# One 512-column matmul for a weight's high part: FFN-in, q/k and gate products with two sums a bank, joined afterwards

## The chip, the core and the metric

The kernel runs on one core of a Trainium2 chip. A core has a matrix engine (PE, with its weight loads shown as PEld), a vector engine (DVE), an activation engine (ACT), GpSimd (POOL), a sync engine that issues the DMAs (SP) and 16 DMA engines. PE writes its sums to eight banks (PSUM), from where ACT and DVE read them. Each engine works its own instructions off in the order in which they stand and waits for the others by semaphores. The metric is the device time of one execution in microseconds, the median of three runs.

## The reference

A trunk of two layers over 256 tokens with 1024 features. Each layer has three sub-layers: a SwiGLU feed-forward (FFN) of width 2816, a mixer of three kinds of attention with gates, and a second FFN. All inputs are float32, and each sub-layer's input is normed, scaled and shifted by vectors that a product of the conditioning vector with `w_ada` gives (adaLN).

```python
h = pre(x, 0)                                   # norm, scale, shift
x = x + 0.5*mod[:,0,2] * swiglu(h, wg, wu, wd)  # (silu(h@wg) * (h@wu)) @ wd
h = pre(x, 1)
(q.., k.., v.., g_sb, g_dil, g_swa) = split(h @ w_in)
merged = sigmoid(g_sb)*(o_sb@w_br_sb) + sigmoid(g_dil)*(o_dil@w_br_dil) + sigmoid(g_swa)*(o_swa@w_br_swa)
x = x + mod[:,1,2] * (merged @ w_out)
h = pre(x, 2)
x = x + 0.5*mod[:,2,2] * swiglu(h, wg2, wu2, wd2)
```

## The kernel before, in words

Every product of float32 operands is made of three: a number is split in a high part of type float32r and a low part, the rest. A product is weight-high by row-high, weight-low by row-high, and weight-high by row-low. The rows' parts are `hH` and `hL`, the weights' are `wH` and `wL`.

The weights stream in as loads of 1 MB, three buffers of them (`RAWS`). A load is cut in units; a unit is a [1024, 128] block of weight columns for FFN-in, q/k and gates. For each unit ACT casts the high part (L149) and DVE subtracts to get the low part (L157). `feed` splits units up to `AHEAD` = 5 in front of the products, and there are `NB` = 6 slots, so a cast also waits until PE is done with the unit six before it.

`step` (L564) writes the program for one unit: first `feed` (the split of the unit five ahead), then adaLN's steps if some are due (L282 on DVE, L280 on ACT, from two load buffers), then the unit's matmuls, then what the unit before left (`pending`), then the unit's own `post`. ACT and DVE get their instructions in this order.

`aform` (L580) makes the matmuls of a unit: eight blocks of 128 features, for each a 256-column matmul with the high and one with the low weight part, then eight more with the rows' low part: 24 of 256 columns. In an FFN, gate and up products of one block of 128 columns share a bank, half each; after the up unit ACT takes the silu of the gate half (L647), DVE multiplies it with the other half (L648), and a step later ACT casts and DVE subtracts the result's parts for the down product (L651, L652). Units go gate, gate, up, up. The first two units of an FFN (other than the first FFN, which has a start of its own, L608) put their products with the rows' low part last.

In the mixer two q/k units share a bank and ACT copies it (L838). Two gate units share a bank and ACT takes the tanh of it (L866). Between the gate units stand the pieces of the attention heads, by a list in `run_mixer`: scores on PE (`pa`, `pb`, `pc`), bias and maxima on DVE (L1046, L1051, L1056), exponentials on ACT (L1066, L1072), division on DVE (L1081, L1088), transposes on PE (`pt`, L1100). After two or four gate units a branch's output product follows (`pb`), and DVE multiplies it with the tanh (L887 to L891).

The down and output products (L701, `pd`) take the tokens as the stationary operand and move 512 or 256 columns of a weight. The six sub-layers are numbered 0 to 5; 1 and 4 are mixers.

Of the kernel before, what the change touches and what calls it, by code (L numbers as in the profile page):

```python
# [16 lines left out]
P = 128  # L17
# [12 lines left out]
# slots of split units, how many of them are split ahead, and slots of loads  # L30
# [3 lines left out]
# units at the end of a sub-layer whose products go piece by piece, and those that the first norm's transposes follow  # L34
# [16 lines left out]
# the last rows' columns on the vector engine; the activation engine takes the others  # L51
# [11 lines left out]
def shape_constants():  # L63
    """One-hot of the bucket of each distance, and the mask of each head by distance (distance 255 - index)."""
# [16 lines left out]
class Unit:  # L81
    """A piece of a weight: `view` picks it from the raw tile of load `raw`; `pe` runs its products."""
# [6 lines left out]
class Trunk:  # L89
# [23 lines left out]
    # ---------------------------------------------------------------- weight stream  # L113
# [23 lines left out]
    def feed(self, ahead=AHEAD, high=0):  # L137
        """Split the units that lie up to `ahead` in front of the products, H one step before L."""
# [26 lines left out]
    # ---------------------------------------------------------------- adaLN  # L165
    def ada_setup(self):
# [11 lines left out]
        # after which sub-layer a sum is reduced, while the next norm runs; the others as they are complete  # L178
# [6 lines left out]
    def first_load(self, q):  # L185
        """Two blocks of columns of the first shift and scale, into what the feed-forward takes later."""
        t = self.sp.tile([P, KB, 2, 256], F32, tag=("bigA", "bigB")[q % 2], name=f"first{q}", bufs=1)
        for kb in range(KB):
            src = self.a["w_ada"][0, kb * P:(kb + 1) * P, 0:2 * D].rearrange("p (c n) -> p c n", c=2)
            self.nc.sync.dma_start(t[:, kb], src[:, :, 256 * q:256 * q + 256])  # L190
        self.first_src[q] = t

    def first_mac(self, q, kbs):
        """Products of some blocks of rows with the vector, on the vector engine."""
# [9 lines left out]
    def first_sum(self, q, kbs, acc=False):  # L204
        """Sums over the rows, of products made here or before: a column tile each for the two blocks of the shift
        and of the scale."""
# [22 lines left out]
    def first_h(self, q, xt, out):  # L229
        """The first norm's output, two blocks of features."""  # L230
# [95 lines left out]
    def ada_reduce(self, ch):  # L326
        """Sums over the partitions on the tensor engine; returns what is left to do.

        A gate is wanted along the free dimension: ones times the products. Shift and scale are wanted along the
        partitions: four column tiles sum a quarter of the columns each, and transposes turn the rows."""  # L330
# [39 lines left out]
    # ---------------------------------------------------------------- constants  # L370
# [69 lines left out]
    # ---------------------------------------------------------------- norm  # L440
    def square(self, t, cols, tag):
        """Mean square over some of the columns."""
# [37 lines left out]
    def norm_pe(self, t, s, xn):  # L480
        """Features to the partitions, one half of them a bank."""
# [9 lines left out]
    def norm_evac(self, t, s, ps, between=()):  # L491
        """Scale and shift by feature, one engine a bank; the high parts too."""
# [33 lines left out]
    def alloc_h(self, s):  # L526
        self.hH = self.sp.tile([P, KB, S], F32R, tag="hH", name=f"hH{s}", bufs=1)
        self.hL = self.sp.tile([P, KB, S], F32R, tag="hL", name=f"hL{s}", bufs=1)
# [11 lines left out]
    def final_gain(self, t, sl):  # L540
        """x times the gain, while the mean square is summed."""
# [21 lines left out]
    # ---------------------------------------------------------------- unit lists  # L563
# [16 lines left out]
    def aform(self, u, out, xh, xl, off=0, part="all"):  # L580
        """out += W^T x for one block of 128 columns of the unit; the products with the low part of x come last."""
# [8 lines left out]

    def col_raw(self, src, widths=((0, 256),)):
        """Load of columns of a [1024, n] weight as [128, 8, 256]."""
# [8 lines left out]
    def plan_ffn(self, l, i, s):  # L601
# [5 lines left out]
        def start_pe(b0, q):  # L607
            """Two blocks of columns over two of rows; both sums of a block share a bank."""  # L608
# [22 lines left out]
        def gate_pe(fb):  # L631
            def pe(u, part="all"):
                if part != "low":
                    ps[fb] = self.ps(f"pf{s}_{fb}")
                self.aform(u, ps[fb][:, :S], self.hH, self.hL, part=part)
            return pe

        def up_pe(fb):
            return lambda u: self.aform(u, ps[fb][:, S:], self.hH, self.hL)

        def up_post(fb):
            def post():
# [6 lines left out]

                def later():  # L650
                    nc.scalar.copy(self.ffH[:, fb, :], f32)  # L651
                    nc.vector.tensor_tensor(self.ffL[:, fb, :], f32, self.ffH[:, fb, :], op=ALU.subtract)  # L652
                return later
# [18 lines left out]
        for q in range(3 if s == 0 else 0, NF // 2):  # L672
            rg, ru = self.col_raw(wg, ((q * 256, 256),)), self.col_raw(wu, ((q * 256, 256),))
            for r, mk in ((rg, gate_pe), (ru, up_pe)):
                for b in range(2):
                    fb = 2 * q + b
                    view = lambda t, b=b: t.rearrange("p (k n) -> p k n", k=KB)[:, :, b * P:(b + 1) * P]
                    u = Unit(r, view, (KB, P), mk(fb), up_post(fb) if r == ru else None)
# [5 lines left out]
    def plan_rows(self, w, nk):  # L684
        """Units of one block of 128 rows of a [n, 1024] weight, two a load."""
# [657 lines left out]
```

## Time and profile before

| what | value |
|---|---|
| median of 3 runs | 1215.85 us (1215.71 to 1215.98) |
| span of the profiled execution | 1213.2 us |
| PE busy | 1184.2 us, 98%, 9005 matmuls |
| DVE busy | 830.4 us, 68% |
| ACT busy | 615.6 us, 51% |
| HBM traffic | 238 GB/s over the span |

The span runs from the first to the last instruction; the rest of a run's time lies around it. The profile's busy time of a matmul contains its way through the array, so that matmuls overlap: how fast they follow one another is read from their starts.

### The profile page before, as it was taken

How to read it: one execution, taken by the hardware profiler on the slowest of the kernel's cores; microseconds unless marked ns; L12 is line 12 of the kernel's file. 1: busy time of each engine (PE TensorE's matmuls, PEld its weight loads, DVE VectorE, ACT ScalarE, POOL GpSimd, SP SyncE). 2: the span in 40 equal slices, each digit the busy share in tenths (PEclk: the TensorE clock that was granted, in tenths of full speed). 3: DMA queues.
4: the chain of work that ended last, by engine and by line, in shares of the span. 5: the costliest groups of instructions: out<-in, count | busy, mean ns of one | idle time of the engine just before them, and what ended most of it. 6: DMA issues, size and time to landing. Idle time of an engine off the chain costs nothing.

```text
span 1213.2 us, 21570 instructions
## 1 busy us (share of the span) xinstructions
PE 1184.2 (98%) x9005; PEld 1115.3 (92%) x9005; DVE 830.4 (68%) x1075; ACT 615.6 (51%) x953; POOL 17.5 (1%) x38
## 2 busy tenths in 40 slices
PE   6999999899999999999999999999999999999997
PEld 5999987799999999999889999889999998999986
DVE  3677576777889897766577667557766788555544
ACT  5555343546564475444365444346655446444432
POOL 1000000000000000000000000000000000000000
PEclk9999999899999999999999999999999999999999
DMA  9999999698779859877739776758843584656550
GB/s 318 308 307 328 266 328 321 205 299 286 249 241 312 310 186 330 253 243 249 251 112 300 217 243 226 257 157 282 269 153 114 180 273 149 199 184 198 174 173 35
DMA packets 189673, 287.58 MB, mean 237 GB/s; under 512 B 6806, under 2 KB 155496, under 8 KB 189576
## 3 DMA queue, kind: packets, MB, share of 16 engines
q1 hardware_dynamic: 187656, 279.88, 69.7%
q0 software_dynamic: 1776, 6.14, 1.8%
q8 instruction: 70, 1.15, 0.4%
q14 instruction: 27, 0.22, 0.1%
q10 hardware_dynamic: 144, 0.20, 0.0%
HBM read 285.12 MB, written 3.42 MB: 238 GB/s over the span
## 4 chain that ended last, share of the span: by engine, by line
PE 85%; DMA 6%; DVE 4%; issue 2%; ACT 2%; POOL 0%; SPq 0%; POOLq 0%; ACTq 0%; DVEq 0%
PE pf L589 36%; PE pd L701 18%; PE pg L589 11%; PE pq L589 7%; DMA ada<-in_w_ada 5%; PE pf L619 3%; PE pb L589 3%; PE pv L934 2%; DVE acc L282 1%; DVE wL L157 1%; PE psn L487 1%; PE adag L343 1%; DMA first<-in_w_ada 1%; DMA raw<-in_w_ffn_gate 0%; ACT wH L149 0%
## 5 line engine op out<-in xcount | busy, mean ns | idle before, releaser
L157 DVE TENSOR_TENSOR wL<-raw,wH 128x1024 fp32r<-128x1024 f32 (+1 forms) x384 | 461.9, 1211 | 223.2 <-ACT wH L149 222.8
L149 ACT CAST wH<-raw 128x1024 fp32r<-128x1024 f32 (+1 forms) x384 | 393.1, 1041 | 243.9 <-PE pd L701 94.7
L589 PE MATMUL pf<-hH,wH 128*128 128x256 f32 x1312 | 323.0, 284 | 0.4 <-DVE hH L504 0.4
L589 PE MATMUL pf<-hH,wL 128*128 128x256 f32 x1312 | 322.0, 283 | 0.0
L589 PEld LDWEIGHTS pf<-hH,wH 128*128 128x128 f32 x1312 | 251.8, 192 | 1.7 <-issue 0.9
L589 PEld LDWEIGHTS pf<-hH,wL 128*128 128x128 f32 x1312 | 251.8, 192 | 0.2 <-issue 0.2
L589 PE MATMUL pf<-hL,wH 128*128 128x256 f32 x1312 | 183.7, 283 | 0.0
L282 DVE SCALAR_TENSOR_TENSOR acc<-ada,sc,acc 128x1024 f32<-128x1024 f32 x112 | 143.4, 1280 | 43.6 <-DMA ada<-in_w_ada 43.5
L589 PEld LDWEIGHTS pf<-hL,wH 128*128 128x128 f32 x1312 | 169.0, 192 | 0.0
L701 PE MATMUL pd<-wL,ffH 128*128 128x512 f32 (+1 forms) x440 | 154.6, 351 | 3.5 <-DVE wL L157 3.5
L701 PE MATMUL pd<-wH,ffH 128*128 128x512 f32 (+1 forms) x440 | 154.6, 351 | 0.0
L701 PE MATMUL pd<-wH,ffL 128*128 128x512 f32 (+1 forms) x440 | 153.6, 349 | 0.0
L701 PEld LDWEIGHTS pd<-wL,ffH 128*128 128x128 f32 x440 | 83.8, 191 | 15.3 <-DVE wL L157 4.7
L589 PE MATMUL pg<-hH,wH 128*128 128x256 f32 x384 | 96.0, 288 | 0.0
L701 PEld LDWEIGHTS pd<-wH,ffH 128*128 128x128 f32 x440 | 84.0, 191 | 12.2 <-issue 0.8
L589 PE MATMUL pg<-hH,wL 128*128 128x256 f32 x384 | 94.0, 283 | 0.0
L701 PEld LDWEIGHTS pd<-wH,ffL 128*128 128x128 f32 x440 | 83.6, 190 | 11.0
L647 ACT ACTIVATE sil<-pf 128x256 f32<-128x256 f32 x88 | 33.4, 383 | 96.6 <-PE pf L589 96.6
L589 PEld LDWEIGHTS pg<-hH,wH 128*128 128x128 f32 x384 | 73.4, 191 | 2.3 <-issue 1.3
L589 PEld LDWEIGHTS pg<-hH,wL 128*128 128x128 f32 x384 | 73.4, 191 | 0.0
L648 DVE TENSOR_TENSOR f<-pf,sil 128x256 f32<-128x256 f32 x88 | 36.9, 422 | 32.9 <-ACT sil L647 32.9
L589 PE MATMUL pq<-hH,wH 128*128 128x256 f32 x224 | 55.8, 287 | 0.0
(204 smaller groups left out, 1390.5 us busy)
## 6 DMA issues: line engine op xcount, KB each, us to landing
ada<-in_w_ada SPq DMA_DIRECT2D x128, 512.0 KB, 5.6
raw<-in_w_ffn_down SPq DMA_DIRECT2D x44, 1024.0 KB, 5.0
raw<-in_w_in SPq DMA_DIRECT2D x42, 1024.0 KB, 6.6
raw<-in_w_ffn_gate SPq DMA_DIRECT2D x41, 1024.0 KB, 6.7
raw<-in_w_ffn_up SPq DMA_DIRECT2D x41, 1024.0 KB, 6.0
first<-in_w_ada SPq DMA_DIRECT2D x32, 256.0 KB, 6.0
raw<-in_w_out SPq DMA_DIRECT2D x8, 1024.0 KB, 6.9
raw<-in_w_ffn_gate SPq DMA_DIRECT2D x12, 256.0 KB, 6.0
```

Source lines behind the costliest of these rows:

```text
L149: nc.scalar.copy(u.H, u.view(self.raw_tiles[u.raw]))
L157: nc.vector.tensor_tensor(u.L, u.view(self.raw_tiles[u.raw]), u.H, op=ALU.subtract)
L282: self.nc.vector.scalar_tensor_tensor(acc, src, sc, acc, ALU.mult, ALU.add)
L343: nc.tensor.matmul(ps[h], self.ones, acc[:, h * 512:(h + 1) * 512], start=True, stop=True)
L487: self.nc.tensor.transpose(p[:, i * P:(i + 1) * P], xn[:, fb * P:(fb + 1) * P], self.ident)
L589: nc.tensor.matmul(out, w[:, kb, cs], x[:, kb, :], start=i == 0, stop=i == n - 1)
L619: self.nc.tensor.matmul(ps[fb][:, S * up:S * up + S], w[:, 2 * k + up, b * P:(b + 1) * P], x[:, 2 * q + k, :], start=q == 0 and not up and ...
L647: nc.scalar.activation(sil, p[:, :S], AF.Silu)
L648: nc.vector.tensor_tensor(f32, p[:, S:], sil, op=ALU.mult)
L701: self.nc.tensor.matmul(out, x[:, kb, sl], w[:, 0, hs], start=first and i == 0, stop=last and i == 2)
L934: self.nc.tensor.matmul(out, x[:, 4 * (i % 2) + k, sl], w[:, k, :], start=i % 2 == 0 and j == 0, stop=i % 2 == 1 and j == n - 1)
```

## The change

The rows' high and low parts now stand side by side in one tile, `hHL`, so that a weight's high part meets [high | low] as one 512-column matmul into a whole bank. The weight's low part times the rows' high part goes on as a 256-column matmul into the bank's first half. A unit then has 8 matmuls of 512 columns and 8 of 256, and two sums in its bank, which `join` adds: ACT copies the second half out, DVE adds the first half. Each unit has a bank of its own and a `post` of its own. This is done for FFN-in (except the first FFN's start), q/k and gates; values, branch outputs, down and output products stay. The first two units of the later FFNs keep 24 matmuls of 256 columns, into two sums. In a gate's post the silu and in the mixer the tanh of two gate units follow the join. (Comments are dropped as well; those lines are left out here.)

```diff
     def alloc_h(self, s):
-        self.hH = self.sp.tile([P, KB, S], F32R, tag="hH", name=f"hH{s}", bufs=1)
-        self.hL = self.sp.tile([P, KB, S], F32R, tag="hL", name=f"hL{s}", bufs=1)
+        self.hHL = self.sp.tile([P, KB, 2, S], F32R, tag="hHL", name=f"hHL{s}", bufs=1)
+        self.hH, self.hL = self.hHL[:, :, 0, :], self.hHL[:, :, 1, :]
...
+    def wide(self, u, bank, part="all"):
+        nc = self.nc
+        one, both = bank[:, :S], bank[:, :]
+        k = u.shape[0]
+        seq = []
+        for kb in range(k):
+            if part == "all":
+                seq += [(both, u.H, self.hHL[:, kb]), (one, u.L, self.hH[:, kb, :])]
+            elif part == "high":
+                seq += [(one, u.H, self.hH[:, kb, :]), (one, u.L, self.hH[:, kb, :])]
+            else:
+                seq += [(bank[:, S:], u.H, self.hL[:, kb, :])]
+        n = len(seq)
+        for i, (out, w, x) in enumerate(seq):
+            kb = i if part == "low" else i // 2
+            rhs = x.rearrange("p c n -> p (c n)") if part == "all" and i % 2 == 0 else x
+            nc.tensor.matmul(out, w[:, kb, :], rhs, start=part != "low" and i == 0, stop=part != "high" and i == n - 1,
+                             skip_group_check=True)
+
+    def join(self, out, bank):
+        self.nc.scalar.copy(out, bank[:, S:])
+        self.nc.vector.tensor_tensor(out, bank[:, :S], out, op=ALU.add)
...
-                self.aform(u, ps[fb][:, :S], self.hH, self.hL, part=part)
+                self.wide(u, ps[fb], part)
             return pe
 
+        def gate_post(fb):
+            def post():
+                sil = self.sil[:, fb % 3, :]
+                self.join(sil, ps[fb])
+                self.nc.scalar.activation(sil, sil, AF.Silu)
+            return post
+
         def up_pe(fb):
-            return lambda u: self.aform(u, ps[fb][:, S:], self.hH, self.hL)
+            def pe(u):
+                ps[fb] = self.ps(f"pu{s}_{fb}")
+                self.wide(u, ps[fb])
+            return pe
+
+        def up_wide_post(fb):
+            def post():
+                f32 = self.f32[:, fb % 3, :]
+                self.join(f32, ps[fb])
+                self.nc.vector.tensor_tensor(f32, f32, self.sil[:, fb % 3, :], op=ALU.mult)
+                return split(fb, f32)
+            return post
...
-                    u = Unit(r, view, (KB, P), mk(fb), up_post(fb) if r == ru else None)
+                    u = Unit(r, view, (KB, P), mk(fb), post(fb))
...
             for u in us:
                 u.pe(u, "low")
+                u.post()
...
         def qk_pe(i):
             def pe(u):
-                if i % 2 == 0:
-                    ps[i // 2] = self.ps(f"pq{s}_{i}")
-                self.aform(u, ps[i // 2][:, (i % 2) * S:(i % 2 + 1) * S], self.hH, self.hL)
+                ps[i] = self.ps(f"pq{s}_{i}")
+                self.wide(u, ps[i])
...
+                self.join(self.qk[:, i, :], ps[i])
...
         def g_post(b, f):
             def post():
-                if f % 4 == 1:
+                if f % 4 == 0:
                     th[b, f // 4] = self.work([P, 4, S], f"th{s}_{b}_{f}")
-                i = f // 2
-                self.nc.scalar.activation(th[b, f // 4][:, 2 * (i % 2):2 * (i % 2) + 2, :],
-                                          gps[b, i].rearrange("p (b n) -> p b n", b=2), AF.Tanh, scale=0.5)
+                t = th[b, f // 4]
+                self.join(t[:, f % 4, :], gps[b, f])
+                if f % 2:
+                    two = t[:, f % 4 - 1:f % 4 + 1, :]
+                    self.nc.scalar.activation(two, two, AF.Tanh, scale=0.5)
             return post
```

The first place is ACT in the FFN-in part of sub-layer 2, column blocks 12 and 13 (`pf` gate, `pu` up). Before, one silu stands for each pair of a gate and an up unit:

```order
L647 ACTIVATE sil2_4787<-pf2_12_5586 128x256
L149 CAST wH158_5674<-raw85_5517 128x1024
L651 CAST ffH2_4785<-f322_4788 128x256
L647 ACTIVATE sil2_4787<-pf2_13_5617 128x256
L149 CAST wH159_5709<-raw85_5517 128x1024
```

Now the same engine at the same blocks reads:

```order
L615 COPY sil2_4392<-pf2_12_5075 128x256
L669 ACTIVATE sil2_4392<-sil2_4392 128x256
L149 CAST wH156_5097<-raw84_4963 128x1024
L615 COPY sil2_4392<-pf2_13_5101 128x256
L669 ACTIVATE sil2_4392<-sil2_4392 128x256
L149 CAST wH157_5121<-raw84_4963 128x1024
L615 COPY f322_4393<-pu2_12_5127 128x256
L149 CAST wH158_5147<-raw85_5018 128x1024
L688 CAST ffH2_4390<-f322_4393 128x256
L615 COPY f322_4393<-pu2_13_5154 128x256
```

The silu has moved from the up unit to the gate unit, behind a copy; it reads the tile that DVE's add writes, and the cast of the next unit's high part stands behind it.

The second place is DVE at the same blocks, now (an add L616 for each unit, a product L682 for each up unit):

```order
L616 TENSOR_TENSOR sil2_4392<-pf2_12_5075,sil2_4392 128x256
L157 TENSOR_TENSOR wL156_5099<-raw84_4963,wH156_5097 128x1024
L616 TENSOR_TENSOR sil2_4392<-pf2_13_5101,sil2_4392 128x256
L157 TENSOR_TENSOR wL157_5123<-raw84_4963,wH157_5121 128x1024
L616 TENSOR_TENSOR f322_4393<-pu2_12_5127,f322_4393 128x256
L682 TENSOR_TENSOR f322_4393<-f322_4393,sil2_4392 128x256
L157 TENSOR_TENSOR wL158_5149<-raw85_5018,wH158_5147 128x1024
```

Before, these blocks had four splits L157 and two products L648 here, and no add. Now a split stands right behind each add, and its `wH` comes from a cast that stands behind the silu of that add.

The third place is ACT in the gate part of the first mixer, at the second branch's first two gate units (`swa1` is the last group of heads). Before:

```order
L149 CAST wH102_3761<-raw54_3508 128x1024
L866 ACTIVATE th1_1_1_3794<-pg1_1_0_3716 128x512
L1101 COPY pT1_swa0_3796<-pt1_swa0_0_3797 128x384
L1072 ACTIVATE p1_swa1_3750,sm1_swa1_3755<-p1_swa1_3750,sm1_swa1_3755 128x256 x3
L1074 ACTIVATE sm1_swa1_3755<-sm1_swa1_3755 128x6
L149 CAST wH103_3819<-raw55_3615 128x1024
```

Now, on DVE, at the same units:

```order
L1104 TENSOR_SCALAR sm1_swa1_3444<-sm1_swa1_3444 128x6
L157 TENSOR_TENSOR wL102_3452<-raw54_3219,wH102_3450 128x1024
L282 SCALAR_TENSOR_TENSOR acc3_0_3367<-ada74_3369,sc_97,acc3_0_3367 128x1024
L616 TENSOR_TENSOR th1_1_0_3427<-pg1_1_1_3459,th1_1_0_3427 128x256
L157 TENSOR_TENSOR wL103_3504<-raw55_3314,wH103_3502 128x1024
L616 TENSOR_TENSOR th1_1_0_3427<-pg1_1_2_3506,th1_1_0_3427 128x256
```

ACT's row of tanh, transposed copies, exponentials and cast is as before, but for two copies more; the tanh now reads what the add L616 writes, which stands behind a split and an adaLN step on DVE. Before, it read the bank that PE wrote.

## Rows read from the trace of the kernel before

**Rows 1.** The page's first part: busy time of the engines.
```profile
PE 1184.2 (98%) x9005; PEld 1115.3 (92%) x9005; DVE 830.4 (68%) x1075; ACT 615.6 (51%) x953; POOL 17.5 (1%) x38
```

**Rows 2.** Busy time by stage: stretch, length, engines, PE clock, DMA share, GB/s.
```profile
145.00:220.00 75.00, 71.46 (x405) 61.04 (x405) 53.76 (x56) 29.91 (x36) 0.00 (x0) 0.95 0.92 325
300.00:405.00 105.00, 104.75 (x867) 100.78 (x866) 94.65 (x128) 58.32 (x104) 0.00 (x0) 1.00 0.81 275
432.00:559.00 127.00, 127.00 (x1059) 126.98 (x1058) 94.25 (x118) 68.19 (x101) 0.00 (x0) 1.00 0.80 267
626.00:753.00 127.00, 127.00 (x1058) 126.91 (x1057) 88.48 (x112) 65.66 (x99) 0.00 (x0) 1.00 0.74 239
886.00:989.00 103.00, 103.00 (x854) 99.96 (x855) 73.23 (x108) 55.64 (x100) 0.00 (x0) 1.00 0.52 168
1017.00:1144.00 127.00, 127.00 (x1057) 126.94 (x1058) 77.20 (x100) 64.49 (x97) 0.00 (x0) 1.00 0.60 191
```

**Rows 3.** The chain that ended last, in order of time: start, us, what.
```profile
124.56 19.34 DMA ada<-in_w_ada
...
325.44 0.04 DVE p_dil L1081
...
326.73 1.18 PE pt_dil L1100 x9
...
432.18 126.82 PE pf L589 x1056
```

**Rows 4.** Timeline of PE in sub-layer 2's down product: start, us, instruction.
```profile
591.26 0.39 PE L701 MATMUL pd<-wH,ffL 128*128 128x512 f32 x1
591.49 0.28 PE L701 MATMUL pd<-wH,ffH 128*128 128x256 f32 x1
591.60 0.28 PE L701 MATMUL pd<-wL,ffH 128*128 128x256 f32 x1
...
592.08 0.28 PE L701 MATMUL pd<-wH,ffL 128*128 128x256 f32 x1
592.20 0.40 PE L701 MATMUL pd<-wH,ffH 128*128 128x512 f32 x1
```

**Rows 5.** Groups by line and shape: busy us, mean ns, idle before.
```profile
L157 DVE TENSOR_TENSOR wL<-raw,wH 128x1024 fp32r<-128x1024 f32 x372 | 451.6, 1223 | 218.3 <-ACT wH L149 217.9
L149 ACT CAST wH<-raw 128x1024 fp32r<-128x1024 f32 x372 | 384.3, 1050 | 242.5 <-PE pd L701 94.7 <-PE pf L589 62.8 <-issue 23.6
...
L648 DVE TENSOR_TENSOR f<-pf,sil 128x256 f32<-128x256 f32 x88 | 36.9, 422 | 32.9 <-ACT sil L647 32.9
...
L866 ACT ACTIVATE th<-pg 128x512 f32<-128x512 f32 x24 | 14.3, 596 | 41.3 <-PE pg L589 40.1 <-issue 1.2
```

**Rows 6.** Timeline of DVE in sub-layer 2's FFN-in.
```profile
489.53 1.28 DVE L282 SCALAR_TENSOR_TENSOR acc<-ada,sc,acc 128x1024 f32<-128x1024 f32 x1
490.73 0.42 DVE L652 TENSOR_TENSOR ffL<-f,ffH 128x256 fp32r<-128x256 f32 x1
491.06 0.42 DVE L648 TENSOR_TENSOR f<-pf,sil 128x256 f32<-128x256 f32 x1
491.40 1.21 DVE L157 TENSOR_TENSOR wL<-raw,wH 128x1024 fp32r<-128x1024 f32 x1
492.53 0.42 DVE L652 TENSOR_TENSOR ffL<-f,ffH 128x256 fp32r<-128x256 f32 x1
```

**Rows 7.** Timeline of ACT, sub-layer 2's FFN-in.
```profile
487.04 0.38 ACT L647 ACTIVATE sil<-pf 128x256 f32<-128x256 f32 x1 [1.78 <-PE pf L589]
487.32 1.04 ACT L149 CAST wH<-raw 128x1024 fp32r<-128x1024 f32 x1
```

**Rows 8.** Timeline of ACT in the first mixer's gate part, two places.
```profile
319.05 0.94 ACT L1066 ACTIVATE p_dil<-p_dil,sm_dil 128x768 f32<-128x768 f32 x1 [2.31 <-DVE sm_dil L1051]
...
320.58 1.03 ACT L149 CAST wH<-raw 128x1024 fp32r<-128x1024 f32 x1
...
350.74 0.51 ACT L1072 ACTIVATE p_swa<-p_swa,sm_swa 128x256 f32<-128x256 f32 x1 [0.83 <-DVE sm_swa L1059]
...
353.49 1.98 ACT L149 CAST wH<-raw 128x1024 fp32r<-128x1024 f32 x2
```

More of the change, by code (lines that the diff above doesn't have):

```diff
@@ L634, in pe, with split, later @@
                     ps[fb] = self.ps(f"pf{s}_{fb}")
-                self.aform(u, ps[fb][:, :S], self.hH, self.hL, part=part)
+                self.wide(u, ps[fb], part)
             return pe
-        def up_pe(fb):
-            return lambda u: self.aform(u, ps[fb][:, S:], self.hH, self.hL)
+        def gate_post(fb):
[4 more added lines that the diff above has]
+            return post
+        def up_pe(fb):
+            def pe(u):
[9 more added lines that the diff above has]
+            return post
+        def split(fb, f32):
+            def later():
+                self.nc.scalar.copy(self.ffH[:, fb, :], f32)
+                self.nc.vector.tensor_tensor(self.ffL[:, fb, :], f32, self.ffH[:, fb, :], op=ALU.subtract)
+            return later
         def up_post(fb):
@@ L648, in post @@
                 nc.vector.tensor_tensor(f32, p[:, S:], sil, op=ALU.mult)
[L650 to L653, printed above, removed]
+                return split(fb, f32)
             return post
@@ L673, in plan_ffn @@
             rg, ru = self.col_raw(wg, ((q * 256, 256),)), self.col_raw(wu, ((q * 256, 256),))
-            for r, mk in ((rg, gate_pe), (ru, up_pe)):
+            for r, mk, post in ((rg, gate_pe, gate_post), (ru, up_pe, up_wide_post)):
                 for b in range(2):
@@ L826, in pe, with qk_post @@
             def pe(u):
-                if i % 2 == 0:
-                    ps[i // 2] = self.ps(f"pq{s}_{i}")
-                self.aform(u, ps[i // 2][:, (i % 2) * S:(i % 2 + 1) * S], self.hH, self.hL)
+                ps[i] = self.ps(f"pq{s}_{i}")
+                self.wide(u, ps[i])
             return pe
-        def qk_post(q):
+        def qk_post(i):
             def post():
                 nc = self.nc
-                p = ps[q]
-                dst = self.qk[:, 2 * q:2 * q + 2, :]
-                src = p.rearrange("p (b n) -> p b n", b=2)
-                nc.scalar.copy(dst, src)
-                if q == 6:
-                    nc.scalar.copy(self.qk[0:64, 14, :], p[64:128, S:])
-                    nc.scalar.copy(self.qk[64:128, 14, :], p[0:64, S:])
+                self.join(self.qk[:, i, :], ps[i])
+                if i == 13:
+                    nc.scalar.copy(self.qk[0:64, 14, :], self.qk[64:128, 13, :])
+                    nc.scalar.copy(self.qk[64:128, 14, :], self.qk[0:64, 13, :])
             return post
@@ L846, in plan_mixer @@
             for b in range(2):
-                u = Unit(r, half(b), (KB, P), qk_pe(2 * q + b), qk_post(q) if b else None)
+                u = Unit(r, half(b), (KB, P), qk_pe(2 * q + b), qk_post(2 * q + b))
                 self.units.append(u)
@@ L855, in pe @@
             def pe(u):
[L856 to L858 removed]
+                gps[b, f] = self.ps(f"pg{s}_{b}_{f}")
+                self.wide(u, gps[b, f])
             return pe
@@ L909, in plan_mixer @@
                     f = f0 + i
-                    u = Unit(r, half(i), (KB, P), g_pe(b, f), g_post(b, f) if i else None)
+                    u = Unit(r, half(i), (KB, P), g_pe(b, f), g_post(b, f))
                     self.units.append(u)
```

3 lines of the change are left out of this document (removed).

## The prediction, made blind

> **What bounds the kernel now.** I read the page's busy times first: PE is busy 98% of the span, DVE 68%, ACT 51% [rows 1]. Then the stages, because DVE's share is an average: in FFN-in parts PE is busy all the time and DVE 77 to 94 of 127 us, but in the first mixer's gate part DVE is busy 94.65 of 105 us, in the second's only 73.23 of 103 [rows 2]. Then the chain of waits. In an FFN-in part it is one piece of PE, 1056 matmuls in 126.82 us, so 120.1 ns from start to start [rows 3]. In the first sub-layer it goes through adaLN's loads (19.34 us in one piece), with the DMA engines at 0.92 [rows 2, 3]. In the first mixer's gate part it passes through DVE's division L1081 at 325.44 and from there to PE's transposes at 326.73 [rows 3]: there DVE already hands over just in time. So the kernel is bound by PE, except in the first sub-layer (DMA) and at the start of the first mixer's gates (DVE).
>
> **What the change removes on PE.** Converted are 158 FFN-in units (32 in sub-layer 0, 42 in each of 2, 3 and 5), 28 of q/k and 48 of gates, 234 in all, each of eight feature blocks. A block had three 256-column matmuls, 3 x 120.1 = 360.3 ns [rows 3]; now it has one of 512 and one of 256, in turn. The down product shows each handover: a 512 followed by a 256 takes 0.23 us, a 256 that comes behind a 512 takes 0.11, and a 256 before a 512 takes 0.12 [rows 4]. The pair is 0.34 to 0.35 us; I take 0.345, a saving of 15 ns a block, 0.12 us a unit, 5.1 us for 42 units, 28 us for all 234. The ends: the times are read to 10 ns, so 0.35 + 0.01 (nothing saved) to 0.34 (20 ns, 37 us for all).
>
> The Trainium skill weighs less: "TensorE: Matmul & The Clock Gate", section Back-to-back issue gap, gives a warm gap of N/2.4 + 2.5 ns for an isolated matmul, an estimate from it being 109.2 ns for 256 columns and 215.8 for 512, so 2.6 ns saved a block and under 5 us in all. The trace disagrees with its level (120.1 and 230 ns), so the sum goes by the rows.
>
> **What it adds.** One ACT copy and one DVE add of 128x256 a converted unit (240 with the two unconverted units of sub-layers 2, 3, 5). No such copy or add from a bank is in the FFN-in of before; the nearest are the silu from a bank, 0.38 us [rows 7], and the product with a bank half, 0.42 us [rows 5]. I take these. Back to back, DVE's instructions follow one another faster than they last: the adaLN step 1.20 us, the split 1.13, a 128x256 one 0.33 to 0.34 [rows 6]; ACT's silu gives way after 0.28 [rows 7].
>
> ACT's copies are cheap: ACT is half idle. What counts is the new wait. Before, the silu and the tanh waited for PE alone. Now each waits for DVE's add, and behind it in ACT's queue stands the cast `wH` of the unit five ahead, for which DVE's very next instruction, the split, waits. So after the add of a gate unit DVE stands idle: silu 0.28, cast 1.05 [rows 5, 7], with two handovers of about 0.03. One round of four units (gate, gate, up, up), when DVE and ACT set the pace: from first to second gate's add 0.31 + 1.08 + split 1.13 + add 0.42, about 2.95 us; from there to the first up's add the same; product 0.37; then split, `ffL`, add and product, 1.13 + 0.33 + 0.45 + 0.34; split, `ffL` and add of the next round, 1.13 + 0.33 + 0.42. Sum 10.4 us, against PE's 4 x 8 x 0.345 = 11.04 (11.53 before). AdaLN's steps come on top.
>
> The splits run five units ahead. In step, `wL` of the unit five ahead is ready about 3.5 us after the unit before ended (copy 0.38, add 0.42, silu 0.28, cast 1.05, split 1.22, handovers), and is needed 5 x 2.76 = 13.8 us after it. So DVE may fall 10.3 us behind before PE waits.
>
> **By stage.**
> - FFN-in of sub-layer 5: no adaLN step. 10.5 rounds x 10.4 = 109.2 on DVE, 115.9 on PE. PE sets the pace: -5.
> - Sub-layer 3: DVE was 88.48 - 77.20 = 11.3 us busier than in sub-layer 5 [rows 2], adaLN's steps. 120.5 against 115.9: 4.6 behind, inside the lead: -5.
> - Sub-layer 2: 94.25 - 77.20 = 17.1 [rows 2]. 126.3 against 115.9: 10.4 behind, the whole lead. I take 2 us of waits: -3. If the round lasts 0.8 us longer than I have it, this becomes +5 and sub-layer 3 about -3.
> - First mixer, gates, 24 units: DVE's 94.65 us [rows 2] plus 24 adds x 0.34 = 8.1; plus 12 tanhs, each with DVE idle for tanh 0.50 to 0.60, cast 1.05 and handovers, 1.65 [rows 5]: 19.8. At four of them the exponentials of a head group stand between tanh and cast, 1.53 us twice and 2.75 twice [rows 8]: 8.6. Before, ACT did these while DVE split. Sum 131 us against 105. The lead doesn't swallow it: PE's transposes come two units behind DVE's division and already met it with nothing to spare [rows 3], and at the end the output product waits for the last splits and the residual behind them. Less 1 us for the branch units' shorter casts: +25, q/k part included, where DVE has room. Ends: +12 if half the idle stretches are filled by what DVE still has to do, +33 if the stalls bring PE below its clock and the w_out rows wait too.
> - Second mixer: few adaLN steps, 73.23 + 8.1 + 28.4 = 109.7 us [rows 2] against PE's 103 - 2.9 = 100.1: 9.6 behind, within the lead but for the transposes. Gates 0, q/k -1.7, the output rows +2.7: +1 (-4 to +8).
> - Sub-layer 0: bound by DMA [rows 2, 3], so PE's 3.9 us are not seen, and late splits free the load buffers later: +2 (-2 to +8).
> - Norms, values and sub-layer ends: same instructions in the same order, 0.
>
> Sum +25 + 1 + 2 - 3 - 5 - 5 = +15 us on a span of 1213.2, so 1228.2; the runs shown lie 2.65 us over the span (1215.85), which gives 1231.
>
> **Rivals.**
> - *The lead swallows it.* The place is the first mixer's gate part. If DVE's idle stretch after a tanh were under about 0.8 us, its sum there, (94.65 + 8.1 + 12 x 0.8), would lie within 10.3 us of PE's 102; then PE's saving would show everywhere but in sub-layer 0: 202 units x 0.12 = 24 us, 1192. For it: PE is busy 104.75 of 105 us there with DVE 90% busy [rows 2]. Against: the order puts a cast of 1.05 us behind every tanh.
> - *Half of it.* Idle stretches lie partly on existing waits; the mixer costs 12: 1218.
> - *No saving on PE.* If a 512-column matmul with its load costs what two of 256 do, sub-layers 3 and 5 give 0, 2 gives +2, the second mixer +4, the first mixer +25, sub-layer 0 +2: +33, 1249. Against it: 0.23 + 0.11 [rows 4]. The Trainium skill's rule above would come near this: about 1246.
> - *Nothing to see.* Saving and stalls cancel, 1216: the stalls would have to be 10 us in the first mixer.
>
> **How the numbers follow.** Chances: the forecast (1222 to 1240) 0.52; half of it 0.14; no saving or longer rounds (1240 to 1255) 0.17; swallowed (1190 to 1210) 0.11; cancelled 0.06. What a measurement can tell from no change is about 0.2%, 2.4 us. Faster: 0.11 and some of the two middle cases, 0.15; same 0.08; slower 0.77. The range 1212 to 1249 leaves out the swallowed case and the upper end of the no-saving case, together about 0.2.
>
> **What would show it.** Right: in FFN-in, pairs of matmuls start 0.34 to 0.35 us apart; DVE's idle before L157 is still put down to ACT's `wH`, with 1.4 us or more after each add of a gate; PE stalls of several us before the transposes in the first mixer, which ends some 25 us later, while FFN-in of sub-layers 3 and 5 shrinks by 5. Wrong: PE without gaps in the first mixer's gates (then the first rival), or FFN-in parts of sub-layer 5 as long as before (then no saving).

## The result, and the profile after

The changed kernel takes 1269.05 us (median of 4 runs, 1267.91 to 1269.21) against 1215.78 us for the kernel before in the same rounds (1215.18 to 1215.98): 1.0437 times as long, 95% interval 1.0423 to 1.0452. The forecast was 1231 us, with a range up to 1249. The sign was right and the size was not: +53 us, where +15 was forecast.

The page's first part, beside [rows 1]:

```profile
PE 1192.6 (94%) x7133; PEld 1022.8 (81%) x7133; DVE 909.1 (72%) x1315; ACT 675.9 (53%) x1179; POOL 18.1 (1%) x38
```

PE's share falls from 98% to 94%: it waits. DVE's busy time grows by 79 us. Where the time went is read from marks, the first start of the matmul `adag` (L343 in both kernels) at the end of sub-layers 0 to 4 (four more `adag` at 119 us, inside sub-layer 0, are left out); the stages s0 to s5 lie between the marks, and the last one ends with the span. This table of stage lengths is worked out from those starts, for the kernel before in us and for every other kernel as the difference to it, each from its profiled execution:

```
                   s0     s1     s2     s3     s4     s5    span
before           228.6  198.5  193.7  193.7  197.7  201.0  1213.2
forecast            +2    +25     -3     -5     +1     -5     +15
after            +17.7  +28.8   +3.8   -2.3   +7.0   -2.0   +53.0
e1_late           +3.5   +1.8   -2.1   -2.2   -2.5   -2.1    -3.6
e2_join_only     +18.6  +26.5   +3.7    0.0   +8.0   +0.2   +57.0
e3_wide_only      -2.0   -2.7   -2.2   -2.2   -2.5   -2.2   -13.8
e4_s0_before      +0.3  +28.4   +3.8   -2.2   +6.9   -2.1   +35.1
e5_one_op        +25.1  +35.6  +14.6   +7.6  +11.8   -2.0   +92.7
e6_late_group     +7.6   +2.2   -3.5   -3.6   -3.2   -3.5    -4.0
e7_late_s0_g      -1.4   +2.0   -2.2   -2.2   -2.5   -2.2    -8.5
e8_late_group_s0  -2.4   -0.2   -3.5   -3.6   -3.2   -3.5   -16.4
e9_no_ada         +3.4   +2.7   -2.2   -2.3   +3.7   -2.6    +2.7
```

From s2 on, stages that should be alike agree within about 0.1 us between kernels (s5 of e9_no_ada is 0.5 off). s0 and s1 move by up to 3 us: e4, e7 and e8 have the same FFN-in of sub-layer 0 and show +0.3, -1.4 and -2.4. Why is not traced, so a difference of that size in s0 or s1 shows nothing. Each row is one execution: those of e6_late_group and e9_no_ada lie at the upper end of their runs (1210.92 of 1206.45 to 1210.92 us; 1217.58 of 1210.15 to 1218.93), those of e7_late_s0_g and e8_late_group_s0 at the lower end. Of the 38 us by which the forecast fell short, s0 has 15.7.

The windows of the changed kernel: FFN-in of sub-layer 0, the first mixer's gates, its output rows, then FFN-in of sub-layers 2, 3 and 5 (columns as in [rows 2]):

```profile
60.00:155.00 95.00, 89.59 (x492) 74.72 (x490) 65.97 (x98) 46.63 (x87) 1.68 (x2) 1.00 0.84 266
317.00:440.00 123.00, 108.79 (x675) 93.89 (x672) 93.17 (x141) 58.56 (x120) 0.00 (x0) 0.94 0.64 215
440.00:474.00 34.00, 29.36 (x133) 23.56 (x132) 27.06 (x38) 16.49 (x29) 0.74 (x2) 0.85 0.76 259
478.00:608.00 130.00, 127.39 (x727) 109.32 (x726) 101.46 (x152) 75.98 (x137) 0.00 (x0) 1.00 0.73 240
676.00:801.00 125.00, 125.00 (x724) 109.21 (x723) 96.39 (x148) 73.84 (x135) 0.00 (x0) 1.00 0.68 227
1072.00:1197.00 125.00, 124.95 (x721) 109.28 (x722) 91.39 (x143) 79.70 (x142) 0.00 (x0) 1.00 0.58 189
```

The first and third of these stretches in the kernel before:

```profile
60.00:155.00 95.00, 95.00 (x778) 93.27 (x777) 65.95 (x86) 44.85 (x71) 1.68 (x2) 1.00 0.95 301
404.00:427.00 23.00, 23.00 (x130) 20.08 (x129) 17.39 (x24) 10.10 (x18) 0.74 (x2) 1.00 0.75 259
```

In sub-layers 3 and 5 PE is busy without a gap, as it was [rows 2], and the stages are 2.0 to 2.3 us shorter. In the gates PE is idle for 14 of 123 us, at a mean granted clock of 0.94. In the output rows about the same matmuls (133 against 130) take 34 us instead of 23, at a mean granted clock of 0.85: PE waits 2.5, 0.8 and 1.4 us there, and in two stretches the clock is at 1.2 GHz instead of 2.4. The first wait, and the two stretches:

```profile
445.40 0.39 PE L748 MATMUL pd<-wH,mHL 128*128 128x256 f32 x1 [2.51 <-DVE mt L935]
446.00:449.40 3.40, 3.40 (x10) 2.63 (x9) 3.40 (x6) 2.11 (x4) 0.00 (x0) 0.50 0.95 375
459.60:466.50 6.90, 6.26 (x15) 4.87 (x16) 6.48 (x7) 1.13 (x2) 0.00 (x0) 0.51 1.00 319
```

Of the 11 us, 6.4 are PE's longer busy time (29.36 - 23.00), the rest are waits.

**The ring in the trace.** DVE and then ACT in sub-layer 2's FFN-in of the changed kernel, two gate units (start, us, instruction, idle time before it and what ended it):

```profile
500.07 0.42 DVE L616 TENSOR_TENSOR sil<-pf,sil 128x256 f32<-128x256 f32 x1
501.92 1.23 DVE L157 TENSOR_TENSOR wL<-raw,wH 128x1024 fp32r<-128x1024 f32 x1 [1.42 <-ACT wH L149]
503.06 0.42 DVE L616 TENSOR_TENSOR sil<-pf,sil 128x256 f32<-128x256 f32 x1
504.90 1.23 DVE L157 TENSOR_TENSOR wL<-raw,wH 128x1024 fp32r<-128x1024 f32 x1 [1.43 <-ACT wH L149]
```

```profile
500.53 0.42 ACT L669 ACTIVATE sil<-sil 128x256 f32<-128x256 f32 x1 [2.32 <-DVE sil L616]
500.85 1.03 ACT L149 CAST wH<-raw 128x1024 fp32r<-128x1024 f32 x1
501.79 0.36 ACT L615 COPY sil<-pf 128x256 f32<-128x256 f32 x1
503.51 0.42 ACT L669 ACTIVATE sil<-sil 128x256 f32<-128x256 f32 x1 [1.36 <-DVE sil L616]
```

Read the two together: the gate's add (L616) starts at 500.07, the silu (L669) 0.46 us later, the cast (L149) behind it at 500.85, the split (L157) at 501.92, the next gate's add at 503.06. ACT waited 2.32 us for the add, then DVE 1.42 us for the cast: the engines take turns. Gate to gate is 2.99 us where the prediction had 2.95. The groups by line, with the idle time before each, show it in sum (before, the silu L647 had waited 96.6 us and the tanh L866 [rows 5] 40.1 us for PE, and neither for DVE):

```profile
L669 ACT ACTIVATE sil<-sil 128x256 f32<-128x256 f32 x82 | 34.3, 418 | 122.1 <-DVE sil L616 122.1
L912 ACT ACTIVATE th<-th 128x512 f32<-128x512 f32 x24 | 15.2, 632 | 84.6 <-DVE th L616 84.6
L157 DVE TENSOR_TENSOR wL<-raw,wH 128x1024 fp32r<-128x1024 f32 x372 | 450.8, 1222 | 234.4 <-ACT wH L149 233.3 <-DMA first<-in_w_ada 0.3
```

L157's own idle time hardly grew (218.3 before); what grew is that it now lies in a loop with ACT's 207 us. A wait that stands in the table with the same sum can be harmless in one kernel and on the path in the other.

### The profile page after: what moved, and what is told of

It reads as the page before. It is cut to its first block, busy times and chain, and to the rows that moved or that the text cites. A ratio compares the mean times of both kernels' runs of the same rounds, so it can differ in the third digit from the quotient of the medians.

```text
span 1266.2 us, 18375 instructions
## 1 busy us (share of the span) xinstructions
PE 1192.6 (94%) x7133; PEld 1022.8 (81%) x7133; DVE 909.1 (72%) x1315; ACT 675.9 (53%) x1179; POOL 18.1 (1%) x38
## 4 chain that ended last, share of the span: by engine, by line
PE 46%; DVE 26%; DMA 10%; ACT 9%; issue 8%; POOL 0%; POOLq 0%; SPq 0%; ACTq 0%; DVEq 0%
PE pd L748 15%; DVE wL L157 11%; PE pf L610 10%; PE pu L610 10%; DMA ada<-in_w_ada 7%; DVE acc L282 5%; ACT wH L149 5%; PE pq L610 3%; PE pg L610 3%; PE pf L646 1%; PE pv L979 1%; DMA first<-in_w_ada 1%; DVE ffL L689 1%; DVE sil L616 1%; DVE f L616 1%
## 5 line engine op out<-in xcount | busy, mean ns | idle before, releaser
L157 DVE TENSOR_TENSOR wL<-raw,wH 128x1024 fp32r<-128x1024 f32 (+1 forms) x384 | 461.2, 1211 | 245.3 <-ACT wH L149 244.2
L149 ACT CAST wH<-raw 128x1024 fp32r<-128x1024 f32 (+1 forms) x384 | 391.3, 1039 | 92.1 <-PE pd L748 56.4
L610 PE MATMUL pu<-hHL,wH 128*128 128x512 f32 x656 | 235.5, 400 | 7.6 <-ACT wH L149 7.4
L610 PE MATMUL pf<-hHL,wH 128*128 128x512 f32 (+1 forms) x704 | 235.0, 384 | 0.4 <-DVE hHL L504 0.4
L610 PE MATMUL pu<-hHL,wL 128*128 128x256 f32 x656 | 186.6, 284 | 3.9 <-DVE wL L157 3.6
L610 PE MATMUL pf<-hHL,wL 128*128 128x256 f32 x656 | 183.0, 282 | 0.4 <-DVE wL L157 0.4
L748 PE MATMUL pd<-wH,ffH 128*128 128x512 f32 (+1 forms) x440 | 155.5, 353 | 1.2 <-DVE sil L616 1.2
L610 PEld LDWEIGHTS pu<-hHL,wH 128*128 128x128 f32 x656 | 124.0, 189 | 37.9 <-ACT wH L149 8.5
L610 PEld LDWEIGHTS pf<-hHL,wH 128*128 128x128 f32 x704 | 129.4, 188 | 29.2 <-issue 0.9
L610 PE MATMUL pg<-hHL,wH 128*128 128x512 f32 x384 | 142.6, 411 | 1.9 <-DVE th L616 1.9
L610 PEld LDWEIGHTS pu<-hHL,wL 128*128 128x128 f32 x656 | 124.8, 190 | 8.6 <-DVE wL L157 8.5
L610 PEld LDWEIGHTS pf<-hHL,wL 128*128 128x128 f32 x656 | 124.3, 189 | 1.3 <-DVE wL L157 1.1
L610 PE MATMUL pg<-hHL,wL 128*128 128x256 f32 x384 | 109.4, 285 | 0.0
L669 ACT ACTIVATE sil<-sil 128x256 f32<-128x256 f32 x82 | 34.3, 418 | 122.1 <-DVE sil L616 122.1
```

The costliest lines, as they stand in the source:

```text
L149: nc.scalar.copy(u.H, u.view(self.raw_tiles[u.raw]))
L157: nc.vector.tensor_tensor(u.L, u.view(self.raw_tiles[u.raw]), u.H, op=ALU.subtract)
L610: nc.tensor.matmul(out, w[:, kb, :], rhs, start=part != "low" and i == 0, stop=part != "high" and i == n - 1, skip_group_check=True)
L669: self.nc.scalar.activation(sil, sil, AF.Silu)
L748: self.nc.tensor.matmul(out, x[:, kb, sl], w[:, 0, hs], start=first and i == 0, stop=last and i == 2)
```

## The experiments

The theory after the result: the price is the order, not the work. Silu and tanh wait for DVE's add, the cast stands behind them, DVE's split behind the cast. Rivals: the added copies and adds as such; the 512-column matmuls or the clock.

**e1_late.** Silu and tanh are issued one step later, behind the cast of the unit five ahead:

```diff
                 self.join(sil, ps[fb])
-                self.nc.scalar.activation(sil, sil, AF.Silu)
+                return lambda: self.nc.scalar.activation(sil, sil, AF.Silu)
...
                     two = t[:, f % 4 - 1:f % 4 + 1, :]
-                    self.nc.scalar.activation(two, two, AF.Tanh, scale=0.5)
+                    return lambda: self.nc.scalar.activation(two, two, AF.Tanh, scale=0.5)
...
                 u.pe(u, "low")
-                u.post()
+                u.post()()
```

> All joins stay; only the silu and the tanh are issued one step later, behind the cast of the unit five ahead. Theory (ring: silu and tanh wait for DVE's add, the cast stands behind them, DVE's split behind the cast): DVE and ACT run past one another again, so sub-layer 0 falls from +17.7 us to +2..+8, the first mixer from +28.8 to +6..+12, the second from +7.2 to 0..+3; sub-layers 2, 3 and 5 gain 2 us each. Sum 1211 to 1232, likeliest 1220. Rival (work: the added copies and adds themselves fill DVE and ACT): no change of more than 5 us from 1269, because not one instruction goes. Rival (PE: the wide matmuls or a lower clock): 1265 to 1270, PE's order is untouched.

Measured: 1211.32 us (7 runs), 0.9962 of before (0.995 to 0.9975), at the lower edge of what was expected: both mixers came out below their ranges. Not one instruction went, and 57 us of span did; the rival by work is out for nearly all of the loss. The waits also cost more than their own length: PE's busy time for the same 7133 matmuls is 1192.6 us in the changed kernel and 1172.9 here, at a mean granted clock of 0.981 against 0.994. By the clock alone some 17 of the 57 us went this way (an estimate, 0.019 x 1266 - 0.006 x 1210, as if PE had had work all the time). DVE and ACT in the same part of e1_late:

```profile
500.95 0.41 DVE L616 TENSOR_TENSOR sil<-pf,sil 128x256 f32<-128x256 f32 x1
501.48 1.23 DVE L157 TENSOR_TENSOR wL<-raw,wH 128x1024 fp32r<-128x1024 f32 x1
```

```profile
500.13 0.38 ACT L615 COPY sil<-pf 128x256 f32<-128x256 f32 x1 [1.09 <-PE pf L610]
500.40 1.05 ACT L149 CAST wH<-raw 128x1024 fp32r<-128x1024 f32 x1
501.40 0.42 ACT L669 ACTIVATE sil<-sil 128x256 f32<-128x256 f32 x1
```

The cast now runs beside the add, the split starts 0.53 us after the add's start instead of 1.85, and ACT waits for PE again. In sum:

```profile
L669 ACT ACTIVATE sil<-sil 128x256 f32<-128x256 f32 x82 | 34.3, 418 | 23.9 <-DVE sil L616 23.9
L912 ACT ACTIVATE th<-th 128x512 f32<-128x512 f32 x24 | 15.2, 632 | 20.8 <-DVE th L616 20.7
L157 DVE TENSOR_TENSOR wL<-raw,wH 128x1024 fp32r<-128x1024 f32 x372 | 451.3, 1221 | 134.0 <-ACT wH L149 130.5
```

**e2_join_only.** The matmuls of before, the join of after:

```diff
-            if part == "all":
-                seq += [(both, u.H, self.hHL[:, kb]), (one, u.L, self.hH[:, kb, :])]
-            elif part == "high":
+            if part != "low":
                 seq += [(one, u.H, self.hH[:, kb, :]), (one, u.L, self.hH[:, kb, :])]
-            else:
-                seq += [(bank[:, S:], u.H, self.hL[:, kb, :])]
+        for kb in range(k if part != "high" else 0):
+            seq += [(bank[:, S:], u.H, self.hL[:, kb, :])]
...
```

> The matmuls are those of before (24 of 256 columns a unit), but the products with the low rows go into a second sum, so the join with its waits is as in the changed kernel. Ring theory: the loss stays and the saving of PE, 7 ns a block or 2.4 us for 42 units, goes: sub-layer 0 +17.7, first mixer +29 to +31, second +8 to +10, sub-layers 2, 3 and 5 between 0 and +6 each; sum 1275 to 1285. Rival (PE: the 512-column matmuls cost the time): back to 1216 to 1225.

Measured: 1273.5 us, 1.0475 (1.0447 to 1.0503), a little under the expected 1275 to 1285. The loss is there without a single 512-column matmul, and in sub-layers 3 and 5 PE's saving is gone (0.0 and +0.2). The rival by matmuls is out.

**e3_wide_only.** The matmuls of after without the join: silu, tanh and copies read the first sum from its bank.

```diff
...
-                self.join(self.qk[:, i, :], ps[i])
+                nc.scalar.copy(self.qk[:, i, :], ps[i][:, :S])
...
-                self.join(t[:, f % 4, :], gps[b, f])
-                if f % 2:
-                    two = t[:, f % 4 - 1:f % 4 + 1, :]
-                    self.nc.scalar.activation(two, two, AF.Tanh, scale=0.5)
+                self.nc.scalar.activation(t[:, f % 4, :], gps[b, f][:, :S], AF.Tanh, scale=0.5)
```

> The matmuls are those of the changed kernel, the join is left out: silu, tanh and copies read the first sum from its bank, so the products of the weights' high parts with the low rows are computed but not added. It gives the saving on PE by itself. From the pair of 353 ns against 3 x 120.1: 7 ns a block, 13 us for 234 units, less the 2 us of sub-layer 0 where DMA sets the pace: 1204 to 1208. By the prediction's pair of 345 ns: 28 us less 4, about 1192. Rival (PE: wide matmuls are slower or bring the clock down): 1216 or more.

Measured: 1201.82 us, 0.9893 (0.9864 to 0.9922); the span is 13.8 us shorter, as 234 x 8 x 7 ns = 13.1 us has it. That is below the 1204 to 1208 expected: I had taken off 2 us for sub-layer 0, and it gains 2.0. Such a gain lies within the scatter of s0; that PE and not DMA set the pace there is read below from the trace of before.

**e4_s0_before.** FFN-in of sub-layer 0 as before (`aform` and the old post for s == 0):

```diff
+                if s in (0,):
+                    return self.aform(u, ps[fb][:, :S], self.hH, self.hL, part=part)
                 self.wide(u, ps[fb], part)
...
```

> FFN-in of sub-layer 0 is as before, the rest as in the changed kernel. If each stage's loss is its own: sub-layer 0 +0 (+-1), the first mixer +27 to +30, sum 1250 to 1253. Rival (carried: sub-layer 0's delay is what the mixer's loss comes from in part, or the mixer's is carried over from late adaLN steps): the first mixer changes by more than 4 us.

Measured: 1250.8 us, 1.0286 (1.0264 to 1.0307), as expected. Sub-layer 0 is back at +0.3 and the first mixer keeps +28.4 of its 28.8: its loss is its own and not carried over from sub-layer 0.

**e5_one_op.** The join as one instruction of DVE, without ACT's copy:

```diff
-        self.nc.scalar.copy(out, bank[:, S:])
-        self.nc.vector.tensor_tensor(out, bank[:, :S], out, op=ALU.add)
+        self.nc.vector.tensor_reduce(out, bank.rearrange("p (c n) -> p n c", c=2), axis=AX.X, op=ALU.add)
```

> As the changed kernel (silu and tanh in their old place), but the join is one instruction on DVE that reads both sums from the bank; ACT's copy and DVE's wait for it are gone, the wait of silu and tanh for DVE stays. If the price is the wait of ACT for DVE with the cast behind it: sub-layer 0 +15 to +20, first mixer +25 to +32, sum 1262 to 1280 (the reduction takes DVE perhaps 0.6 us instead of 0.35). Rival (DVE's wait for ACT's copy is half of it): the first mixer falls by 8 us or more and the sum below 1250.

Measured: 1308.38 us, 1.0752 (1.0729 to 1.0775), far above what I expected. The 0.6 us for the reduction in it was a guess; the group shows 684 ns where the add took 418:

```profile
L615 DVE TENSOR_REDUCE sil<-pf 128x256 f32<-128x512 f32 x82 | 55.8, 684 | 0.0
```

In sub-layer 2, 42 x 0.266 = 11.2 us, and the stage grew by 10.8 over the changed kernel; in sub-layer 3 by 9.9. Where DVE sets the pace, its added time counts nearly one for one. Sub-layer 5, without adaLN's steps, did not change. The copy and DVE's wait for it are gone here, and what that brings in those two stages is at most the 0.4 to 1.3 us that are missing from 11.2: they were not the price.

**e6_late_group.** e1_late, with the eight 512-column matmuls of a unit ahead of the eight of 256:

```diff
+        if part == "all":
+            seq = seq[::2] + seq[1::2]
...
```

> As e1_late, and within a unit the eight 512-column matmuls come first, then the eight of 256 columns. It measures the handovers of the pair: alternating, a 256 starts 0.235 us behind a 512 and a 512 0.118 behind a 256, 5.65 us for two units. If each kind takes its own time (0.229 and 0.120 from the down product and from before) a unit takes 2.79 instead of 2.83 us, 7 us for 234 units less what sub-layer 0 and the first mixer hide: 1205 to 1208. Rival (the price sits in the weights' loads, whatever the order): 1210 to 1213.

Measured: 1209.36 us, 0.9931 (0.9912 to 0.995). Two units, in the chain of waits of the changed kernel and of this one:

```profile
1083.95 5.66 PE pf L610 x32
```

```profile
1033.87 5.59 PE pu L612 x32
```

A piece of 32 matmuls is two units of eight blocks: 5.59 / 16 = 349 ns a block; alternating, 353. The stages 2, 3 and 5 gain 1.4 us each over e1_late, as expected (42 x 8 x 4 ns = 1.3). Sub-layer 0 lost 4.1 us more than in e1_late in the profiled execution, which I have not explained; the total came out above the 1205 to 1208 expected.

**e7_late_s0_g.** e1_late, with FFN-in of sub-layer 0 and the first mixer's gates as before (the edit of e4, and for the gates the same with s == 1; the matmuls of the gates are shown):

```diff
+                if s in (1,):
+                    gps[b, f] = self.ps(f"pg{s}_{b}_{f}") if f % 2 == 0 else gps[b, f - 1]
+                    return self.aform(u, gps[b, f][:, (f % 2) * S:(f % 2 + 1) * S], self.hH, self.hL)
...
```

> As e1_late, but FFN-in of sub-layer 0 and the gates of the first mixer are as before; wide products stay in sub-layers 2, 3 and 5, in q/k and in the second mixer's gates. If the 3.5 and 1.8 us that e1_late still loses are DVE's added work where DVE has no room: sub-layer 0 0 to +0.5, first mixer -1.5 to 0, the rest as in e1_late (-2.1, -2.2, -2.5, -2.1); sum 1205 to 1208. Rival (the order alone costs it): within 2 us of e1_late, 1209 to 1212.

Measured: 1208.77 us, 0.993 (0.9915 to 0.9945), between what was expected (up to 1208) and its rival (from 1209). Sub-layer 0 gave back its 3.5 us and 1.4 more. The first mixer did not: +2.0, as with converted gates. So nothing points to the gates' adds as what e1_late still loses there; the scatter of s1 is as large as the 2 us at stake.

**e9_no_ada.** The changed kernel with its posts in their old place, without adaLN's multiply-adds on DVE:

```diff
-        else:
+        elif i < 16:
             self.nc.vector.scalar_tensor_tensor(acc, src, sc, acc, ALU.mult, ALU.add)
```

> The changed kernel with its posts in their old place, but the 112 multiply-adds of adaLN on DVE (1.2 us each, from the third sum on) are left out; the loads stay. It takes from DVE the work that comes on top of the ring of copy, add, silu, cast and split. If a stage loses only what the ring and the steps together exceed PE's time and the lead by: sub-layer 0 -2 to 0, first mixer 0 to +8 (21 steps go, 25 us), sub-layer 2 -2.2, second mixer 0 to +3, sub-layers 3 and 5 as they were; sum 1208 to 1222. Rival (each wait of the ring reaches PE directly, whatever else DVE has to do): sub-layer 0 +10 or more, first mixer +20 or more, sum above 1245.

Measured: 1215.14 us (10 runs), 0.9989 (0.9972 to 1.0006), no different from before and inside what was expected. The ring is all there, but with 1.2 us less of other work per step most of the loss is gone: sub-layer 2 has PE's full saving (-2.2), the first mixer falls from +28.8 to +2.7, the second, with few such steps, from +7.0 to +3.7. So a stage loses what ring and steps together exceed PE's time and its lead by. Sub-layer 0 keeps 3.4 us, against -2 to 0 expected; there the chain goes through a load:

```profile
124.30 24.40 DMA raw<-in_w_ffn_up
```

**e8_late_group_s0.** The version that the runs point to: e6_late_group with FFN-in of sub-layer 0 as before.

> Meant as the version that beats both: silu and tanh one step later, the 512-column matmuls of a unit ahead of those of 256, FFN-in of sub-layer 0 as before. From the stages of the runs so far: sub-layer 0 -1.4 to +0.3, first mixer +1 to +2.2, then -3.5, -3.6, -3.2, -3.5; sum 1202 to 1206. Rival (what sub-layer 0 gives back is lost again in the first mixer): 1207 to 1210, as e6_late_group.

Measured: 1205.3 us (7 runs, 1198.87 to 1208.77), 0.9916 (0.9898 to 0.9934): faster than the changed kernel, and faster than before by 0.8%, as expected. The edits are those above, together:

```diff
+                if s in (0,):
+                    return self.aform(u, ps[fb][:, :S], self.hH, self.hL, part=part)
...
+            seq = seq[::2] + seq[1::2]
...
+                return lambda: self.nc.scalar.activation(sil, sil, AF.Silu)
...
```

The profiled execution is the fastest of the seven, so its stages 0 and 1 in the table are on the good side; what makes these runs differ by 10 us stays open.

## Why the prediction was right in sign and wrong in size

**What bounds the kernel.** Right for FFN-in and the first mixer. Wrong for sub-layer 0, the largest miss: "bound by DMA [rows 2, 3], so PE's 3.9 us are not seen, and late splits free the load buffers later: +2". I read this from a window, 145 to 220, that lies mostly in the down product, and from an adaLN load that is in the chain only from 124.56 on. In FFN-in itself PE was busy for 95.00 of 95 us, and most of the chain there is one piece of PE:

```profile
60.89 48.95 PE pf L589 x408
```

DVE waited 4.4 and 5.7 us for adaLN's loads in that stretch and PE did not stop. The prediction's own sum, had I made it there, gives 8 rounds x 10.4 + 13 adaLN steps x 1.20 (counted between 60 and 155) = 98.8 us against PE's 8 x 11.3 = 90.4, 8.4 us behind. That is inside the lead of 10.3; but DVE's delay is handed on, because a load is issued when its buffer comes free, and DVE then waits for that load with the next splits behind the wait. The same long adaLN load in the chain of the changed kernel, and of e1_late:

```profile
135.93 19.43 DMA ada<-in_w_ada
```

```profile
125.27 20.06 DMA ada<-in_w_ada
```

It began at 124.56 before [rows 3]: DVE came to the step that frees its buffer 11.4 us late, the load took as long as ever, DVE waited for it, and PE ran out of split weights behind that. In the changed kernel:

```profile
155.38 1.28 DVE L282 SCALAR_TENSOR_TENSOR acc<-ada,sc,acc 128x1024 f32<-128x1024 f32 x1 [7.43 <-DMA ada<-in_w_ada]
158.78 0.79 PE L610 MATMUL pu<-hHL,wH 128*128 128x512 f32 x1 [7.43 <-ACT wH L149]
```

FFN-in ended 11.2 us later (first start of `pd` 166.7 against 155.5), and what follows up to the mark added 6.5. So the loads did matter, but through DVE's queue, and what was lost is PE's time.

**PE's saving.** The term of 15 ns a block was mis-sized: 7 ns. The two handovers that I read to 10 ns each, 0.23 and 0.11 to 0.12, are 0.235 and 0.118 in the changed kernel:

```profile
1119.83 0.40 PE L610 MATMUL pf<-hHL,wH 128*128 128x512 f32 x1
1120.07 0.28 PE L610 MATMUL pf<-hHL,wL 128*128 128x256 f32 x1
1120.19 0.40 PE L610 MATMUL pf<-hHL,wH 128*128 128x512 f32 x1
```

A closer reading of before would not have said it: over all its down and output products a 512 followed by a 256 takes 227 ns on average and a 256 before a 512 a median of 120, so 13 ns saved. That the two take more when they alternate all the time only the changed kernel shows; 7 lay within the ends I gave (0 to 20 ns). The missing 8 ns a block are 2.7 us of the miss in each of sub-layers 2, 3 and 5 and 2.4 in the second mixer, some 10 us of the 38. The Trainium skill, "TensorE: Matmul & The Clock Gate", section Back-to-back issue gap, would have given 2.5 ns a block by its formula for an isolated matmul, an estimate. Measured is 7 (e3_wide_only, 13.8 us), between the two.

**The ring.** Right, and right in size. Forecast for a round 10.4 us; measured between two like places of the chain, 11.69 us with one adaLN step in between (1.20), so 10.5:

```profile
527.69 1.23 DVE wL L157
528.92 1.19 DVE acc L282
...
539.38 1.23 DVE wL L157
540.61 1.20 DVE acc L282
```

The idle time of "1.4 us or more after each add of a gate" is 1.42 and 1.43.

**The lead.** The step "DVE may fall 10.3 us behind" took DVE to start level with PE, and that failed in sub-layer 2. By the forecast's sum with the measured pair, sub-layer 2 would be 126.3 - 118.6 = 7.7 us behind, inside the lead; it lost 6.0 (3.8 + 2.2). But part of the lead is spent before the first unit: PE had the first gates' sums at 484.3, and DVE, with the norm's last rows, four splits and the gate's sums ahead, came to the first add at 487.87:

```profile
L610 PE MATMUL pu<-hHL,wH x176: 387/396/507, 484.3 to 607.4; 128*128 128x512 f32 x176
```

```profile
482.12 4.63 DVE L157 TENSOR_TENSOR wL<-raw,wH 128x1024 fp32r<-128x1024 f32 x4
486.67 1.28 DVE L348 TENSOR_TENSOR gate<-adag,gate 128x512 f32<-128x512 f32 x2
487.87 0.41 DVE L616 TENSOR_TENSOR sil<-pf,sil 128x256 f32<-128x256 f32 x1
```

The first up unit's add already stands 6 us behind the end of its matmuls, and PE's first wait comes when the adds are some 12 us behind (the unit that ended at 532.4 has its add at 544.71):

```profile
487.06 0.28 PE L610 MATMUL pu<-hHL,wL 128*128 128x256 f32 x1
493.15 0.42 DVE L616 TENSOR_TENSOR f<-pu,f 128x256 f32<-128x256 f32 x1
533.15 0.39 PE L610 MATMUL pu<-hHL,wL 128*128 128x256 f32 x1 [0.36 <-DVE wL L157]
544.71 0.42 DVE L616 TENSOR_TENSOR f<-pu,f 128x256 f32<-128x256 f32 x1
```

So the lead's size was about right, and 6 + 7.7 us do not fit into it. From 532.4 on PE falls behind its pace in 12 places, 4.3 us in sum: FFN-in takes 129.4 us, against 124.7 in sub-layer 3, and the down product behind it 1.3 us longer than before. Sub-layer 3, 120.5 - 118.6 = 1.9 us behind by the same sum, also starts with 6 us, ends with some 10, and PE never waits.

**The first mixer.** Forecast +25 (12 to 33), measured +28.8: the mechanism is right, and that the size is too is in part luck, because two misses cancel. The sum had put all of it, 131 - 105 us, into the gates; they lost 18.5 (104.2 to 122.7 us from the first `pg` to the end of the last `pb`). The output rows lost 10.4, which stood in the upper end alone. The rest: q/k -0.9, ahead of it +0.8. The transposes wait as foretold (us in total, times, longest):

```profile
PE pt_dil L1145 <- DVE p_dil L1126: 6.5, 2, 5.0
PE pt_swa L1145 <- DVE p_swa L1133: 5.8, 2, 4.7
```

Only the upper end had a lower clock in it; it came, at the output rows and, with a mean of 0.94, in the gates. **The second mixer**: +7.0 where +1 was taken, inside its -4 to +8: gates +4.6 instead of 0 (the 9.6 us behind were to lie within the lead; PE waits 3.3 and 0.9 us before the transposes there), output rows +3.3 instead of +2.7, q/k -0.9 instead of -1.7.

**In sum.** Of the 38 us, sub-layer 0 has 15.7 and PE's smaller saving 10.5; with that taken out, the first mixer has 3.8, sub-layer 2 4.1 and the second mixer 3.6.

**The rivals.** "The lead swallows it" and "half of it" fell with the mixer. "No saving on PE" named 1249 and was nearer to the time, but for another reason: PE did save, and sub-layer 0 lost far more than the +2 of that rival.

**What is left of the price.** Against e3_wide_only, e1_late still loses 5.5 us in sub-layer 0 and 4.5 in the first mixer, and nothing elsewhere. In sub-layer 0 it goes when the conversion does (e7, e8). In the first mixer, PE's waits that e3_wide_only does not have are 1.8 us before the transposes `pt_dil`, 0.3 before `pt_swa` and 1.2 before the next norm's transposes, 3.3 of the 4.5; e7_late_s0_g has others (1.4 before `po`, 0.8 before `pt_dil`). No experiment separates them.

## What to carry to other kernels

An operation that moves from "reads what PE wrote" to "reads what another engine wrote" ties two in-order queues together, and the price is not its own time but that of whatever stands behind it: look what is queued there and issue that first. Here the same instructions in another order are worth 57 us. Sum such a ring in every stage against that stage's own row, FFN-in by the FFN-in window and not by its neighbour. Look where each engine stands when the stage begins before a lead is counted on. And when DVE's progress issues the loads, count its delay as handed on, not as hidden by the DMA.

## What the hardware showed that I had not expected

- With a weight load for each, float32r matmuls of 512 and 256 columns take 349 ns a pair in rows of one kind (5.59 us for 16 pairs), but 235 + 118 = 353 ns in turn: 4 ns a pair for alternating (e6_late_group).
- DVE's reduction over two values from a bank, 128x256 out of 128x512, takes 684 ns, against 418 for the add of 256 columns (e5_one_op).
- In the first mixer's output rows, with waits of 2.5, 0.8 and 1.4 us, the mean granted clock was 0.85, against 1.00 before, and PE was busy 6.4 us longer with about the same matmuls. In FFN-in of sub-layer 2, with 2.6 us of idle time in 130, it stayed at 1.00.
